# Attention scores by three 64-row products per head, in the two halves of TensorE's array

## The chip, the core and the metric

The program runs on one NeuronCore of a Trainium2 chip. TensorE (PE) multiplies matrices: the stationary operand is loaded into its array of 128 rows and columns by a weight load (PEld), and the moving operand streams past, one column at a time. VectorE (DVE), ScalarE (ACT) and GpSimd (POOL) work elementwise, SyncE (SP) issues transfers. The metric is device time in microseconds (us) of one execution of the whole program; lower is better.

## What is computed

One step of a two-layer decoder trunk on 1024 prompt tokens and 8 sample tokens, width 1024. The first layer mixes tokens by dilated window attention: three groups g with window and dilation (128, 1), (512, 4), (2048, 16), 16 heads of 64 each; the groups are merged per head by their softmax denominators. Then come a gated channel mixer, a pooling mixer, and a second channel mixer; neither these nor the samples' attention change. What the change touches is this, per block of 128 queries of a residue stream:

```python
s = jnp.einsum("nbqhd,nbkhd->nbhqk", qb, kb).astype(jnp.float32) * SCALE
s = s + bias[:, np.clip(rel, 0, SPAN)]
s = jnp.where(valid[None, :, None], s, NEG_INF)
m = jnp.max(s, axis=-1)
p = jnp.exp(s - m[..., None])
l = jnp.sum(p, axis=-1)
o = jnp.einsum("nbhqk,nbkhd->nbqhd", p.astype(v.dtype), vb).astype(jnp.float32)
```

A block of queries reads the keys of its own block and, where there is one, of the block before.

## The kernel before

All matrix products are made of rounded parts: an operand is split into its rounded value and the rest, and three products (value by value, value by rest, rest by value) are added in PSUM.

`order` lists 24 **units**, a pair of heads (hp) in a group (g), pair by pair with g = 2, 1, 0. While a unit's queries, keys and values are projected, the attention of the unit before runs in between. The projections of a unit are nine groups of 24 products of 336 to 352 columns (`accumulate`, L116), three chunks of tokens for each of queries, keys and values. Behind every third product `between` is called; it moves a clock on by one place, 72 in a unit, and issues the steps of the list `plan` that have come due. So the order on each engine is fixed when the program is written: a step's instructions stand on every engine's queue in the order of the places, and an instruction that waits holds up all behind it on that engine. `attend` puts block i's scores at place 6i+1, the transposes of its weights (`probs_t`) at 6i+15, weights times values (`pv`) at 6i+24, and `finish_o` two places behind each second block. Steps of the sample tokens and of the merge of the groups (`behind`, `extra`) lie between these.

- `evacuate` (L353 on) copies a projected chunk from PSUM to the tile `raw` on ScalarE (L362), queries scaled by 1/8, in the order of the residue streams.
- `pack_q` (L384) makes of a head's queries a tile of 128 rows: rounded values in the head's own 64 rows and their rests in the other 64. `pack_k` (L398) makes a tile of keys twice over and, beside it, keys' rests over 64 rows of zeros. Both are copies and subtractions of 64 partitions by 512, on ScalarE, VectorE and GpSimd, at places 29 to 46.5 and 50 to 59.
- `scores` (L441): a **narrow** block (no block before it; 13 of the 24 blocks of a pair) is one product per head of 256 columns (keys, and keys' rests; L450), and VectorE adds the two halves and the bias (L451). A **wide** block is two products per head of 256 columns, added in PSUM (L457). Then VectorE adds the rest and takes the row maximum (L459), negates it (L461), and ScalarE takes the exponential (L463). The scores of both heads share one bank of PSUM (`s`).
- `probs_t` transposes the weights into one bank (`pt`, L471, L473); ScalarE rounds them (L475) and VectorE takes the rest (L476).
- `pv_mm` (L483) streams the weights' two parts in one product of 256 or 512 columns per head, into columns of their own; two of the three banks `o` hold the two heads of a pair of blocks. `finish_o` waits for ScalarE's copy across partitions (L501), adds on VectorE (L510), and GpSimd adds the two parts into token order (L518).

## Time and profile before

| | us |
|---|---|
| median of 3 runs (lowest to highest) | 3011.26 (3010.56 to 3012.93) |
| span of the profiled execution | 3007.3 |
| of it TensorE busy | 2796.5 |
| VectorE busy | 1649.7 |
| ScalarE busy | 1273.2 |
| GpSimd busy | 1241.8 |

The span runs from the first to the last instruction; the 4 us between it and the median lie around it. Matmul records overlap, as a product's end is modelled with its way through the array; what a product costs in a stream is read from one start to the next. A row "X <- Y" of waits says that X's engine sat idle until Y was done.

### The profile page before, as it was taken

Reading aid. Unit: us, or ns where it says so; the run is one execution under the profiler, and the core shown is the slowest. Engines: PE = TensorE matmul, PEld = TensorE weight load, DVE = VectorE, ACT = ScalarE, POOL = GpSimd, SP = SyncE. Lnnn points to the kernel's source line nnn. Section 1 sums busy time; section 2 is a strip of 40 time slices with the busy share of each in tenths; the row PEclk is TensorE's granted clock in tenths of the full one; section 3 lists DMA queues with packets and bytes.
Section 4 is the critical chain, followed back from the end, with each engine's and each line's share of the span. In section 5 each row is a group of like instructions: output and inputs, shape, how many; then the busy total and the mean of one; then the engine's idle time right before and its main releaser. Section 6 shows DMA issues by size and latency. Waiting matters only on the chain.

```text
span 3007.3 us, 45367 instructions
## 1 busy us (share of the span) xinstructions
PE 2796.5 (93%) x17677; PEld 2724.2 (91%) x17677; DVE 1649.7 (55%) x3338; ACT 1273.2 (42%) x2596; POOL 1241.8 (41%) x949
## 2 busy tenths in 40 slices
PE   7998999998989898899999999998797999999998
PEld 5988888888989798889999999998787999999998
DVE  6677767676777767766222222337977422223235
ACT  5565656565656555544312122224454221312222
POOL 4345554555354636444423232336543532323231
PEclk9999999999999999999999999999898999999999
DMA  3134332433232324356111111113225211111111
GB/s 114 54 86 115 82 85 78 109 100 89 70 111 82 103 54 127 130 146 54 63 44 50 44 48 50 47 66 110 88 88 60 90 50 43 50 50 43 50 43 60
DMA packets 190119, 227.38 MB, mean 76 GB/s; under 512 B 68736, under 2 KB 152560, under 8 KB 189904
## 3 DMA queue, kind: packets, MB, share of 16 engines
q1 hardware_dynamic: 189856, 224.47, 26.9%
q8 instruction: 139, 2.28, 0.3%
q14 instruction: 76, 0.62, 0.1%
q10 hardware_dynamic: 48, 0.02, 0.0%
HBM read 201.55 MB, written 23.34 MB: 75 GB/s over the span
## 4 chain that ended last, share of the span: by engine, by line
PE 50%; DVE 10%; ACT 2%; issue 2%; DMA 1%; POOL 1%; SPq 0%; DVEq 0%; ACTq 0%; POOLq 0%
PE mm L116 49%; DVE nm L461 1%; DVE conv L1108 1%; POOL w_lo L96 1%; DVE sums L1217 1%; DVE part L211 1%; DMA w_raw<-in_w_in 1%; DVE p L459 0%; DVE nrow L239 0%; ACT w_hi L95 0%; DVE hl L251 0%; DVE x L393 0%; ACT p L463 0%; DVE k L402 0%; DVE phl L476 0%
## 5 line engine op out<-in xcount | busy, mean ns | idle before, releaser
L116 PE MATMUL mm<-hh,w_hi 128*128 128x352 f32 (+2 forms) x4064 | 1347.5, 332 | 29.4 <-DVE conv L1099 9.7
L116 PE MATMUL mm<-hh,w_lo 128*128 128x352 f32 (+2 forms) x4064 | 1316.5, 324 | 5.7 <-POOL w_lo L96 5.5
L116 PE MATMUL mm<-hl,w_hi 128*128 128x352 f32 (+2 forms) x4064 | 1318.3, 324 | 3.4 <-DVE hl L251 3.2
L116 PEld LDWEIGHTS mm<-hh,w_hi 128*128 128x128 f32 x4064 | 780.6, 192 | 40.3 <-DVE conv L1099 10.2
L116 PEld LDWEIGHTS mm<-hl,w_hi 128*128 128x128 f32 x4064 | 780.6, 192 | 10.5 <-DVE hl L251 6.8
L116 PEld LDWEIGHTS mm<-hh,w_lo 128*128 128x128 f32 x4064 | 779.2, 192 | 7.2 <-POOL w_lo L96 7.2
L96 POOL TENSOR_TENSOR w_lo<-w_raw,w_hi 128x1024 fp32r<-128x1024 f32 x194 | 478.2, 2466 | 530.7 <-ACT w_hi L95 515.4
L1108 DVE SCALAR_TENSOR_TENSOR conv<-gate,convp,conv 128x1024 f32<-128x1024 f32 (+3 forms) x126 | 135.0, 1072 | 474.8 <-ACT conv L1106 463.2
L116 PE MATMUL mm<-gh,w_hi 128*128 128x352 f32 (+2 forms) x1056 | 338.8, 321 | 7.8 <-ACT gh L1100 7.6
L116 PE MATMUL mm<-gl,w_hi 128*128 128x352 f32 (+2 forms) x1056 | 339.0, 321 | 1.2 <-POOL gl L1101 1.2
L116 PE MATMUL mm<-gh,w_lo 128*128 128x352 f32 (+2 forms) x1056 | 338.5, 321 | 0.2 <-POOL w_lo L96 0.2
L1044 DVE TENSOR_TENSOR x<-x,mm 128x352 f32<-128x352 f32 (+2 forms) x312 | 159.0, 511 | 309.0 <-PE mm L116 308.8
L95 ACT ACTIVATE w_hi<-w_raw 128x1024 fp32r<-128x1024 f32 x196 | 205.5, 1051 | 242.4 <-PE mm L116 231.3
L463 ACT ACTIVATE p<-p,nm 128x128 f32<-128x128 f32 (+1 forms) x384 | 169.8, 443 | 296.3 <-DVE nm L461 286.1
L1101 POOL TENSOR_TENSOR gl<-conv,gh 128x352 fp32r<-128x352 f32 (+2 forms) x132 | 122.5, 939 | 269.4 <-ACT gh L1100 267.6
L116 PEld LDWEIGHTS mm<-gh,w_hi 128*128 128x128 f32 x1056 | 199.2, 189 | 8.6 <-ACT gh L1100 8.1
L96 POOL TENSOR_TENSOR w_lo<-part,w_hi 128x1024 fp32r<-128x1024 f32 x56 | 138.2, 2468 | 151.5 <-ACT w_hi L95 142.1
L116 PEld LDWEIGHTS mm<-gl,w_hi 128*128 128x128 f32 x1056 | 199.0, 188 | 1.8 <-POOL gl L1101 1.8
L476 DVE TENSOR_TENSOR phl<-pt,phl 128x512 fp32r<-128x512 f32 (+1 forms) x192 | 104.6, 545 | 173.8 <-ACT phl L475 172.5
L116 PEld LDWEIGHTS mm<-gh,w_lo 128*128 128x128 f32 x1056 | 199.2, 189 | 0.5 <-POOL w_lo L96 0.5
L362 ACT ACTIVATE raw<-mm 128x336 f32<-128x336 f32 (+1 forms) x216 | 144.2, 669 | 118.4 <-PE mm L116 115.8
L1090 ACT ACTIVATE gate<-mm 128x352 f32<-128x352 f32 (+2 forms) x132 | 60.0, 455 | 299.6 <-PE mm L116 299.6
(195 smaller groups left out, 3467.6 us busy)
## 6 DMA issues: line engine op xcount, KB each, us to landing
w_raw<-in_w_in SPq DMA_DIRECT2D x76, 512.0 KB
w_raw<-in_w_qkv SPq DMA_DIRECT2D x72, 512.0 KB
part<-in_w_in SPq DMA_DIRECT2D x38, 512.0 KB
w_raw<-in_w_out SPq DMA_DIRECT2D x36, 512.0 KB
x<-qd SPq DMA_DIRECT2D x48, 256.0 KB
kc<-in_cache_k SPq DMA_DIRECT2D x48, 256.0 KB
vc<-in_cache_v SPq DMA_DIRECT2D x48, 256.0 KB
x<-c_d SPq DMA_DIRECT2D x42, 256.0 KB
```

The lines of the kernel that those rows point to most:

```text
L95: nc.scalar.activation(hi, raw, AF.Copy)
L96: (eng or nc.gpsimd).tensor_sub(lo, raw, hi.bitcast(F32))
L116: nc.tensor.matmul(ps, l, r, start=first and i == 0, stop=last and i == n - 1)
L211: self.engines[j].tensor_add(acc, acc, s[:, :self.w])
L362: nc.scalar.activation(stream(raw[:, :T], u.g, c0, t1, which > 0), ps[:, :w].rearrange("p (s r) -> p s r", r=DILS[u.g]), AF.Copy, scale=scale)
L461: nc.vector.tensor_scalar(nm, u.st[:, i, :, 0], -1.0, None, op0=ALU.mult)
L463: nc.scalar.activation(p[:, h, :w], p[:, h, :w], AF.Exp, bias=nm[:, h:h + 1], accum_out=u.st[:, i, h, 1:2])
L476: nc.vector.tensor_sub(phl[:, :, 1, :w], ps[:, :, :w], phl[:, :, 0, :w].bitcast(F32))
L1044: nc.vector.tensor_add(xT[ct][:, c0:c1], xT[ct][:, c0:c1], ps)
L1090: nc.scalar.activation(gate[:, 2 + s:2 + e], group(tiles8(w, c), c), AF.Copy)
L1101: nc.gpsimd.tensor_sub(self.gl[f][:, s:e], conv[:, s:e], self.gh[f][:, s:e].bitcast(F32))
L1108: nc.vector.scalar_tensor_tensor(conv[:, c0:t1], gate[:, j + c0:j + t1], cw[j], conv[:, c0:t1], op0=ALU.mult, op1=ALU.add)
```

## The change

The tile of keys becomes one for both heads: 128 partitions, that is 64 of each head, with values and rests side by side. Queries are no longer packed: `evacuate` writes the rounded, negated queries from PSUM on ScalarE and their rests from PSUM on VectorE, straight into a pair of tiles, of which there are two (`queries`, `other_queries`) for odd and even units. A block's scores are three products per head of 64 rows, head A in rows 0 to 63 of the array and head B in rows 64 to 127, in turn, each head into a bank of its own. Scores, bias table and masks are negated, so that the reduction takes a minimum and the exponential a scale of -1; L451 and L461 go. `pv_mm` adds the weights' two parts in PSUM, as two products of half the columns; both heads share one bank and two banks take turns; `finish_o` adds on VectorE straight into token order, and GpSimd's addition goes. Banks of PSUM: `s` from one to two, `o` from three to two.

The program has as many transfers on SyncE's queue as before. The diff, without lines that only change comments, placeholders of the norms' banks, or line numbers:

```diff
-        keys = [qp.tile([128, 2, T], F32R, name=f"k{h}") for h in range(2)]
+        keys = qp.tile([128, 2, T], F32R, name="k")
+        other_queries = qp.tile([128, 2, T], F32R, name="q")
+        queries = []
...
-                    nc.vector.tensor_add(masks[g], ps, masks[g])
+                    nc.vector.scalar_tensor_tensor(masks[g], ps, -1.0, masks[g], op0=ALU.mult, op1=ALU.subtract)
...
-            nc.scalar.activation(stream(raw[:, :T], u.g, c0, t1, which > 0),
-                                 ps[:, :w].rearrange("p (s r) -> p s r", r=DILS[u.g]), AF.Copy, scale=scale)
+            src = ps[:, :w].rearrange("p (s r) -> p s r", r=DILS[u.g])
+            if which == 0:
+                hi, lo = (stream(raw[x], u.g, c0, t1, False) for x in range(2))
+                nc.scalar.activation(hi, src, AF.Copy, scale=-scale)
+                nc.vector.scalar_tensor_tensor(lo, src, -scale, hi.bitcast(F32), op0=ALU.mult, op1=ALU.subtract)
+            else:
+                nc.scalar.activation(stream(raw[:, :T], u.g, c0, t1, True), src, AF.Copy)
...
-        def pack_q(u):
-            raw = u.raw[0]
-            if not queries:
-                queries.extend(x_row(h, F32R)[:, :T] for h in range(2))
-
-            def part(h, own, other, t):
-                (nc.vector.tensor_copy(queries[h][own, t], raw[own, t]) if h else
-                 nc.scalar.activation(queries[h][own, t], raw[own, t], AF.Copy))
-                (nc.vector if h else nc.gpsimd).tensor_sub(queries[h][other, t], raw[own, t],
-                                                           queries[h][own, t].bitcast(F32))
-
-            return parts(part, (0, T // 2))
-
         def pack_k(u):
             raw = u.raw[1]
 
-            def part(h, own, other, t):
-                nc.vector.tensor_copy(keys[h][own, 0, t], raw[own, t])
-                nc.scalar.activation(keys[h][other, 0, t], raw[own, t], AF.Copy)
-                (nc.vector if h else nc.gpsimd).tensor_sub(keys[h][own, 1, t], raw[own, t],
-                                                           keys[h][own, 0, t].bitcast(F32))
-
-            return parts(part, (T // 2, 0))
-
-        def parts(f, starts):
-            return [partial(f, h, own, other, slice(t, t + T // 2)) for t in starts
-                    for h, (own, other) in enumerate(((A, B), (B, A)))]
-
+            def part(eng, t):
+                nc.scalar.activation(keys[:, 0, t], raw[:, t], AF.Copy)
+                eng.tensor_sub(keys[:, 1, t], raw[:, t], keys[:, 0, t].bitcast(F32))
+            return [partial(part, nc.vector, slice(T // 2, T)), partial(part, nc.gpsimd, slice(0, T // 2))]
...
-            ps = app.tile([128, 2, 2, 128], F32, name="s", tag="s")
+            ps = [app.tile([128, 256], F32, name="s", tag="s", bufs=2)[:, :w] for h in range(2)]
             p = qp.tile([128, 2, 256], F32, name="p", tag="p", bufs=4)
-            nm = qp.tile([128, 2], F32, name="nm", tag="nm", bufs=2)
-            if w == 128:
-                for h in range(2):
-                    nc.tensor.matmul(ps[:, h], queries[h][:, q], keys[h][:, :, k], start=True, stop=True)
-                nc.vector.tensor_add(p[:, :, :w], ps[:, :, 0], u.bias[:, :, :w])
-                s, bias = ps[:, :, 1], p
-            else:
-                s, bias = ps.rearrange("p h a q -> p h (a q)"), u.bias
-                for h in range(2):
-                    for x in range(2):
-                        nc.tensor.matmul(s[:, h], queries[h][:, q], keys[h][:, x, k], start=x == 0, stop=x == 1)
+            for j, (x, y) in enumerate(((0, 0), (0, 1), (1, 0))):
+                for h, own in enumerate((A, B)):
+                    nc.tensor.matmul(ps[h], u.raw[0][x][own, q], keys[own, y, k], start=j == 0, stop=j == 2)
             for h in range(2):
-                nc.vector.tensor_tensor_reduce(p[:, h, :w], s[:, h, :w], bias[:, h, :w], 1.0, -3e38,
-                                               op0=ALU.add, op1=ALU.max, accum_out=u.st[:, i, h, 0:1])
-            nc.vector.tensor_scalar(nm, u.st[:, i, :, 0], -1.0, None, op0=ALU.mult)
+                nc.vector.tensor_tensor_reduce(p[:, h, :w], ps[h], u.bias[:, h, :w], 1.0, 3e38,
+                                               op0=ALU.add, op1=ALU.min, accum_out=u.st[:, i, h, 0:1])
             for h in range(2):
-                nc.scalar.activation(p[:, h, :w], p[:, h, :w], AF.Exp, bias=nm[:, h:h + 1],
+                nc.scalar.activation(p[:, h, :w], p[:, h, :w], AF.Exp, bias=u.st[:, i, h, 0:1], scale=-1.0,
                                      accum_out=u.st[:, i, h, 1:2])
...
-                nc.tensor.matmul(u.o[h][:, :, 128 * q:128 * (q + b1 - b0)], u.v[j // 4][:, j % 4, h, :],
-                                 u.pt[j][0][:, h, :, 128 * b0:128 * b1], start=first, stop=True, skip_group_check=True)
+                for x in range(2):
+                    nc.tensor.matmul(u.o[:, h, 128 * q:128 * (q + b1 - b0)], u.v[j // 4][:, j % 4, h, :],
+                                     u.pt[j][0][:, h, x, 128 * b0:128 * b1], start=first and h + x == 0, stop=True,
+                                     skip_group_check=True)
...
-                u.o = [app.tile([128, 2, 256], F32, name="o", tag="o", bufs=3) for h in range(2)]
+                u.o = app.tile([128, 2, 256], F32, name="o", tag="o", bufs=2)
...
-                x = 512 * (j // 2 % 2)
-                tmp = (part[:, 0, x:x + 512].rearrange("p (x q) -> p x q", x=2) if (u.hp, u.g) != order[23] else
-                       qp.tile([128, 2, 256], F32, name="ot", tag="ot", bufs=1))
+                x = 256 * (j // 2 % 2)
+                tmp = (part[:, 0, x:x + 256] if (u.hp, u.g) != order[23] else
+                       qp.tile([128, 256], F32, name="ot", tag="ot", bufs=1))
                 u.tmp = tmp, u.o
                 for h, (own, other) in enumerate(((A, B), (B, A))):
-                    nc.scalar.activation(u.tmp[0][own], u.o[h][other], AF.Copy)
+                    nc.scalar.activation(tmp[own], u.o[other, h], AF.Copy)
...
             tmp, o = u.tmp
+            if u.g == 0:
+                dst, split = u.og[:, 256 * i:256 * i + 256], lambda t: t
+            elif u.g == 1:
+                dst = u.og.rearrange("p (n q r) -> p r n q", n=2, r=4)[:, i]
+                split = lambda t: t.rearrange("p (n q) -> p n q", n=2)
+            else:
+                dst = u.og.rearrange("p (s r) -> p r s", r=16)[:, 4 * i:4 * i + 4]
+                split = lambda t: t.rearrange("p (n q) -> p n q", n=4)
             for h, own in enumerate((A, B)):
-                nc.vector.tensor_add(tmp[own], o[h][own], tmp[own])
-            if u.g == 0:
-                dst, split = u.og[:, 256 * i:256 * i + 256], "p q -> p q"
-            elif u.g == 1:
-                dst, split = u.og.rearrange("p (n q r) -> p r n q", n=2, r=4)[:, i], "p (n q) -> p n q"
-            else:
-                dst, split = u.og.rearrange("p (s r) -> p r s", r=16)[:, 4 * i:4 * i + 4], "p (n q) -> p n q"
-            parts = [tmp[:, x] if u.g == 0 else tmp[:, x].rearrange(split, n=2 if u.g == 1 else 4) for x in range(2)]
-            nc.gpsimd.tensor_add(dst, *parts)
-
+                nc.vector.tensor_add(dst[own], split(o[own, h]), split(tmp[own]))
...
-                nc.vector.tensor_max(mx, top[:, 0], top[:, 1])
-                nc.vector.tensor_max(mx, mx, top[:, 2])
-                nc.vector.tensor_sub(e, top, each(mx))
+                nc.vector.tensor_tensor(mx, top[:, 0], top[:, 1], op=ALU.min)
+                nc.vector.tensor_tensor(mx, mx, top[:, 2], op=ALU.min)
+                nc.vector.tensor_sub(e, each(mx), top)
...
-                        self.rooms = [[keys[x][:, :, t:t + 256] for x in range(2)] for t in (768, 512)]
+                        self.rooms = [[other_queries[:, x, t:t + 512].rearrange("p (b d) -> p b d", b=2) for x in range(2)]
+                                      for t in (0, 512)]
...
-                    u.raw.append(qp.tile([128, NT], F32, name="raw", tag="raw", bufs=RAW))
+                    if which:
+                        u.raw.append(qp.tile([128, NT], F32, name="raw", tag="raw", bufs=RAW))
+                    elif n % 2:
+                        if not queries:
+                            queries.extend(x_row(x, F32R)[:, :T] for x in range(2))
+                        u.raw.append(queries)
+                    else:
+                        u.raw.append([other_queries[:, x] for x in range(2)])
...
-                if n and i in (2, 5):
-                    places = (29, 29 + 3, 44.5, 44.5 + 2) if i == 2 else [50 + 3 * j for j in range(4)]
-                    plan.extend(zip(places, pack_q(u) if i == 2 else pack_k(u)))
+                if n and i == 5:
+                    plan.extend(zip((50, 53), pack_k(u)))
```

Two places show the order. On TensorE, in the attention of a unit of g = 0, from the values of one block to the scores of the next; o are weights times values, s scores, pt transposed weights, mm the projection. Before:

```order
L483 MATMUL o<-phl,vhl 128x2x128 x2
L116 MATMUL mm<-hh,w_hi 128x352
L116 MATMUL mm<-hl,w_hi 128x352
L116 MATMUL mm<-hh,w_lo 128x352
L457 MATMUL s<-k_100,x_593 128x256 x2
L457 MATMUL s<-k_101,x_594 128x256 x2
L116 MATMUL mm<-hh,w_hi 128x336
L116 MATMUL mm<-hl,w_hi 128x336
L116 MATMUL mm<-hh,w_lo 128x336
```

and after:

```order
L463 MATMUL o<-phl,vhl 128x128 x4
L116 MATMUL mm<-hh,w_hi 128x352
L116 MATMUL mm<-hl,w_hi 128x352
L116 MATMUL mm<-hh,w_lo 128x352
L436 MATMUL s<-k,q 128x256 x6
L116 MATMUL mm<-hh,w_hi 128x336
L116 MATMUL mm<-hl,w_hi 128x336
L116 MATMUL mm<-hh,w_lo 128x336
```

The steps stand at the same places between the same large products; two products of the values have become four of half the columns, and four of the scores six with 64 rows.

On VectorE, in the attention of a unit of g = 2, where the next unit's queries (x) and keys (k) are packed from raw; phl are rests of the weights, part and o the sums of the values, ks the samples' keys. Before:

```order
L365 TENSOR_SCALAR ks_98<-mm_4336 128x8
L391 CAST x1_594<-raw_3983 64x512
L393 TENSOR_TENSOR x1_594<-raw_3983,x1_594 64x512
L402 CAST k0_100<-raw_4174 64x512
L476 TENSOR_TENSOR phl_4427<-pt_4424,phl_4427 128x2x128
L402 CAST k1_101<-raw_4174 64x512
L404 TENSOR_TENSOR k1_101<-raw_4174,k1_101 64x512
L510 TENSOR_TENSOR part_65<-o_4408,part_65 64x512
L510 TENSOR_TENSOR part_65<-o_4409,part_65 64x512
```

and after:

```order
L373 TENSOR_SCALAR ks_98<-mm_4384 128x8
L396 TENSOR_TENSOR k_100<-raw_4217,k_100 128x512
L454 TENSOR_TENSOR phl_4474<-pt_4471,phl_4474 128x2x128
L499 TENSOR_TENSOR x6_4319<-o_4455,part_65 64x4x64 x2
L454 TENSOR_TENSOR phl_4516<-pt_4513,phl_4516 128x2x128
L499 TENSOR_TENSOR x6_4319<-o_4528,part_65 64x4x64 x2
```

The copies and rests of queries and keys ahead of the rests of the weights (phl) have left this place but for one subtraction of keys; the sums of the values write the output row (x6) themselves. The queries' rests stand earlier, behind each chunk of the queries' projection.

## Rows read from the trace of the kernel before

**Rows 1.** The page's part 1, the whole span: busy us of each engine (share of the span) xinstructions.

```profile
PE 2796.5 (93%) x17677; PEld 2724.2 (91%) x17677; DVE 1649.7 (55%) x3338; ACT 1273.2 (42%) x2596; POOL 1241.8 (41%) x949
```

**Rows 2.** The stretch in which attention runs beside the products of the projections, 60 to 1330 us: busy time of each engine with its count of instructions in brackets, the granted clock of TensorE as a share, the share of DMA and GB/s; and, of the same stretch, the longest waits of TensorE: who waited for whom, us in total, times, longest us.

```profile
60.00:1330.00 1270.00, 1144.76 (x7349) 1089.72 (x7349) 910.53 (x2175) 737.78 (x1766) 612.52 (x418) 0.97 0.34 94
...
PE pt L471 <- DVE phl L476: 37.6, 35, 2.6
PE o L483 <- DVE part L510: 37.5, 23, 3.3
PE spv L760 <- DVE so L787: 14.2, 10, 2.5
```

**Rows 3.** The same view of two units' stretches: one that carries steps of the sample tokens, and the one behind it, which carries none.

```profile
691.80:745.70 53.90, 45.65 (x298) 42.45 (x299) 39.24 (x89) 30.82 (x76) 33.36 (x20) 1.00 0.31 78
745.70:792.50 46.80, 45.01 (x297) 43.65 (x297) 32.29 (x74) 27.10 (x70) 15.89 (x12) 1.00 0.16 45
```

**Rows 4.** TensorE's groups of instructions, whole span, shapes kept apart: stationary x moving shape, count | busy us, mean ns of one | idle before. L450 and L457 are scores, L483 is weights times values.

```profile
L450 PE MATMUL s<-k,x 128*128 128x256 f32 x208 | 42.7, 286 | 3.0 <-POOL k L404 2.9
L457 PE MATMUL s<-k,x 128*128 128x256 f32 x352 | 56.1, 281 | 1.3 <-DVE st L459 1.3
L483 PE MATMUL o<-phl,vhl 128*128 128x256 f32 x304 | 68.3, 293 | 31.2 <-DVE part L510 30.6
L483 PE MATMUL o<-phl,vhl 128*128 128x512 f32 x128 | 43.2, 409 | 6.8 <-DVE part L510 6.8
```

**Rows 5.** Pieces of TensorE's order of time in a unit without samples: start us, us (of a merged row, of all of it), engine, line, operation. The first piece is a narrow block of scores between large products, the second four transposes, the third weights times values and then a wide block of scores.

```profile
756.00 0.32 PE L116 MATMUL mm<-hh,w_lo 128*128 128x352 f32 x1
756.16 0.40 PE L450 MATMUL s<-k,x 128*128 128x256 f32 x2
756.39 0.33 PE L116 MATMUL mm<-hh,w_hi 128*128 128x352 f32 x1
756.56 0.32 PE L116 MATMUL mm<-hl,w_hi 128*128 128x352 f32 x1
...
758.13 0.32 PE L116 MATMUL mm<-hh,w_lo 128*128 128x352 f32 x1
758.29 0.60 PE L434 MATMUL vt<-consts,raw 128*128 128x128 f32 x4
758.64 0.41 PE L116 MATMUL mm<-hh,w_hi 128*128 128x352 f32 x1
758.89 0.33 PE L116 MATMUL mm<-hl,w_hi 128*128 128x352 f32 x1
...
759.54 0.32 PE L116 MATMUL mm<-hh,w_lo 128*128 128x352 f32 x1
759.71 0.40 PE L483 MATMUL o<-phl,vhl 128*128 128x256 f32 x2
759.94 0.32 PE L116 MATMUL mm<-hh,w_hi 128*128 128x352 f32 x1
760.10 0.32 PE L116 MATMUL mm<-hl,w_hi 128*128 128x352 f32 x1
760.26 0.32 PE L116 MATMUL mm<-hh,w_lo 128*128 128x352 f32 x1
760.42 0.63 PE L457 MATMUL s<-k,x 128*128 128x256 f32 x4
760.89 0.31 PE L116 MATMUL mm<-hh,w_hi 128*128 128x336 f32 x1
761.04 0.32 PE L116 MATMUL mm<-hl,w_hi 128*128 128x336 f32 x1
```

**Rows 6.** Order of time around four small products of 16 rows (L783), the only ones of this stretch that use a part of the array's rows: weight loads (PEld) and products (PE), with the large products ahead and behind.

```profile
391.44 0.32 PE L116 MATMUL mm<-hh,w_lo 128*128 128x344 f32 x1
391.68 0.52 PEld L783 LDWEIGHTS spt<-selm,spv_sb 16*128 16x128 f32 x4 [0.21 <-issue]
...
392.22 0.19 PEld L116 LDWEIGHTS mm<-hh,w_hi 128*128 128x128 f32 x1
392.22 0.42 PE L116 MATMUL mm<-hh,w_hi 128*128 128x344 f32 x1
392.32 0.19 PEld L116 LDWEIGHTS mm<-hl,w_hi 128*128 128x128 f32 x1
...
392.48 0.31 PE L116 MATMUL mm<-hl,w_hi 128*128 128x344 f32 x1
```

**Rows 7.** From the same piece of time, a GpSimd instruction and a VectorE one.

```profile
391.83 2.35 POOL L594 TENSOR_TENSOR x<-x,x 128x1024 f32<-128x1024 f32 x1
...
392.32 1.88 DVE L461 TENSOR_SCALAR nm<-st 128x2 f32<-128x2 f32 x1
```

**Rows 8.** VectorE's costliest groups in the stretch of 60 to 1330 us that the diff touches, shapes kept apart: count | busy us, mean ns of one | idle before.

```profile
L510 DVE TENSOR_TENSOR part<-o,part 64x512 f32<-64x512 f32 x184 | 126.2, 686 | 7.1 <-ACT part L501 3.8
L461 DVE TENSOR_SCALAR nm<-st 128x2 f32<-128x2 f32 x192 | 107.3, 559 | 6.7
L402 DVE CAST k<-raw 64x512 fp32r<-64x512 f32 x96 | 79.4, 828 | 2.3
L393 DVE TENSOR_TENSOR x<-raw,x 64x512 fp32r<-64x512 f32 x48 | 71.0, 1479 | 1.6
L404 DVE TENSOR_TENSOR k<-raw,k 64x512 fp32r<-64x512 f32 x48 | 67.6, 1408 | 1.6
```

More of the change, by code (lines that the diff above doesn't have):

```diff
@@ L302, in place @@
             banks.rotate(1)
-            return app.tile([128, 512], F32, name="nstat", tag=banks[0], bufs=3 if banks[0] == "o" else 1)
+            return app.tile([128, 512], F32, name="nstat", tag=banks[0], bufs=2 if banks[0] in "os" else 1)
         nc.scalar.activation(warm, ones, AF.Sqrt)
-        banks = deque(["o", "o", "pt", "misc", "o", "s"])
+        banks = deque(["o", "o", "pt", "misc", "s", "s"])
         load_x(0)
@@ L326, in step @@
             def step(g, tag, src):
-                ps = app.tile([16, TAB], F32, name="btp", tag=tag)
+                ps = app.tile([16, TAB], F32, name="btp", tag=tag, bufs=2 if tag == "s" else 1)
                 ps = ps[:, :src.stop - src.start]
@@ L353, in trunk @@
         class Unit:
+            pass
         def evacuate(u, which, ps, c):
@@ L936, in trunk @@
                             b2 = qp.tile([128, 2, 128], F32, name=f"bias2_{x}")
-                            nc.gpsimd.memset(b2, NEG)
+                            nc.gpsimd.memset(b2, -NEG)
                             bias2.append(b2)
@@ L940, in trunk @@
                         nc.gpsimd.memset(zero, 0.0)
-                        for h, other in enumerate((B, A)):
-                            nc.scalar.activation(keys[h][other, 1], zero[other].to_broadcast([64, T]), AF.Copy)
                         nc.scalar.activation(pst.rearrange("p g b c -> p (g b c)"), zero.to_broadcast([128, 48 * NS]), AF.Copy)
@@ L954, in trunk @@
                         later(f, .8)
-                if n == 0 and i in (6, 7):
+                if n == 0 and i == 7:
                     nc.scalar.activation(warm, ones, AF.Exp)
-                    for f in pack_q(u) if i == 6 else pack_k(u):
+                    for f in pack_k(u):
                         later(f, .6)
```

1 line of the change is left out of this document (removed).

## Prediction

> **What bounds the kernel now.** First the page's busy times: TensorE is busy in 93% of the span and VectorE in little over half [rows 1], so the end is set by TensorE's queue: a step is worth what it puts on that queue or how long it makes it wait. The diff touches only the stretch with attention, so I read that next. Of its 1270 us TensorE is busy 1144.8 and idle 125.2, with a granted clock of 0.97; the longest waits are all for VectorE: transposes wait until the rests of the weights before them have left their bank (37.6), values wait for a free sum bank (37.5), samples' products wait 14.2 [rows 2]. VectorE is busy 72% of this stretch, more than its share of the whole. Then units beside each other: one with samples' steps idles 8.25 of 53.9 us, the next, without them, 1.8 of 46.8 us at clock 1.00, though VectorE is busy 69% in it too [rows 3]. So the kernel here is TensorE's stream plus VectorE's queueing. The change trades one for the other: it takes much from VectorE and adds products to TensorE.
>
> **Prices on TensorE's queue.** I read a step's price from starts: from the large product ahead to the second one behind, less the two large products themselves (0.31 to 0.33). Then a narrow block of scores, two products of 256 columns, costs 0.24; four transposes of 128 columns 0.44; the values, twice 256 columns, 0.24; a wide block, four products of 256, 0.46 [rows 5]. A product of 128 columns thus takes 0.11 and one of 256 only 0.12: with few columns the weight load sets the pace. The load's own length says so too: the four of 16 rows run in 0.52 together, one each 0.11, whether or not rows are filled [rows 6]. Streaming 256 columns more adds 0.116 to a product (409 against 293 ns [rows 4]), so 128 columns stream in 0.06.
>
> **Weights times values.** 304 products of 256 columns (152 pairs) [rows 4] become 608 of 128, each paced by its load: 608 x 0.11 - 152 x 0.24 = +30.4 us. 128 products of 512 become 256 of 256: four at 0.12 are 0.48 against 2 x (0.12 + 0.116) = 0.47, +0.6. Together **+31**, all of it on TensorE's queue, since the large products leave no hole.
>
> **Scores.** 208 / 2 = 104 narrow blocks and 352 / 4 = 88 wide ones [rows 4] become six products each. No row shows 64 rows of the array. The nearest are the four small products of 16 rows: the first load starts 0.24 after the large product ahead, which otherwise is followed after 0.16, and the first large product behind starts only with its own load, 0.26 ahead of the next [rows 6]. In all the four cost 392.48 - 391.44 - 0.31 = 0.73, of which four loads are 0.44: **0.29 is the price of going over to part of the array and back**, and the last product then also has to stream before the array is given back (0.06 or 0.12). I take 0.29 for 64 rows, the nearest row; the other end is 0, if it came from those few rows alone.
>
> What the trace doesn't show is whether two halves load and stream side by side. At one end the six products are three turns: narrow 3 x 0.11 + 0.06 + 0.29 = 0.68, wide 3 x 0.11 + 0.12 + 0.29 = 0.74, that is 104 x 0.44 + 88 x 0.28 = +70 us. At the other end they are six: narrow 1.01, wide 1.07, or 104 x 0.77 + 88 x 0.61 = +134. I take **+70**: the two halves share no row of the array, no partition they read and no bank they write, and in the rows a load waits only for another load into the same rows. The Trainium skill (TensorEngine Tiling (Array Packing), section Tiling Modes) says that different tiles can load weights and multiply in parallel; by that the sum is the one I take, else the 64 us more of the six turns, and no run here shows it.
>
> **VectorE, ScalarE and GpSimd.** Gone from VectorE in this stretch: sums of the values 126.2, negated maxima 107.3, keys 79.4 and 67.6, queries' rests 71.0 [rows 8], 451 us, and with them smaller copies and additions. The negated maxima are 128 x 2 elements; their mean of 559 ns is mostly waiting. One of them lasts 1.88 us and ends at 394.20, as the GpSimd instruction that began before it ends at 394.18 [rows 7]. That work comes back smaller: 192 sums of half the columns (0.34 to 0.69 each by the 686 ns of L510, 66 to 131 us), 72 rests of queries (at most 0.69, so 50), 24 rests of keys (at most 1.41, so 34). VectorE loses some 240 to 350 of its 910.5 us and falls from 72% to about half of the stretch. ScalarE loses copies and GpSimd packing and final sums; neither is waited for above. SyncE's queue keeps its transfers.
>
> **What the waits give back.** The idle time is 125.2. A quiet unit keeps 1.8 [rows 3]; 24 such are 43, the one end, and 0 the other. I keep 35, near the quiet unit, which still had the old VectorE work: **-90** (-82 to -125). The wait for a sum bank should go wholly, since a bank now waits two pairs of blocks for its turn. Late next are the samples' chains through one bank and back, whose steps stay. The clock: 0.97, a mean of its two levels of 2.4 and 1.2 GHz, over 1270 us [rows 2] withholds 38 us of full clock, the quiet unit gets 1.00; part of the withheld time is itself idle, so **-22** (-10 to -38). The queries' new rests add a wait: a bank of the projection is free only after ScalarE and then VectorE have read it. Behind that subtraction stand the next blocks' row maxima and rests of weights. TensorE has two such banks and fills one in 24 products of 0.16, 3.8 us, which covers two reads of under 0.8; I cost it at nothing. If that cover is gone and each of the 72 chunks waits for one VectorE instruction of 0.69 [rows 8], that is 50 us, within the range below.
>
> **Sum.** +31 + 70 - 90 - 22 = -11. The profiled span is 3007.3; the median 3011.26 has 4 us more around it, and these don't change. Predicted time **3000 us**. By its own bounds this case reaches from 2950 (waits and clock given back in full) to 3025 (least given back, some of the bank's wait).
>
> **Rivals.**
> 1. *Six turns:* the halves load one behind the other, as each load does in every row so far [rows 5, 6]. +31 + 134 - 112 = +53: **3064**, slower. It decides the sign from where a pair takes more than 0.13 us (11 us over 192 x 3 pairs is 0.02 each). For it: every load shown has a turn of its own. Against it: all of these are loads into the same rows.
> 2. *No price for the change of array part:* 192 blocks x 0.29 = 56 us less than the forecast: **2944**. For it: the 0.29 is read from products of 16 rows and 4 columns alone. Against it: its two gaps lie outside those products, one ahead and one behind.
> 3. *A load can't run under a product in its own rows:* then each of the three turns is load and stream in series, narrow 3 x 0.17 + 0.29 = 0.80, wide 3 x 0.23 + 0.29 = 0.98; 104 x 0.56 + 88 x 0.52 = 104 us: +31 + 104 - 112 = +23, **3034**. Against it: the load at 392.32 starts while the large product of 392.22 runs in the same 128 rows [rows 6]. The Trainium skill (TensorE: Matmul & The Clock Gate, section Part 3: Packing small matmuls — row/col tiling) says that a load overlaps products in flight only where the row groups differ, which would give this time; for full rows the row here speaks against it.
> 4. *The waits stay:* the idle time hangs on the chain from ScalarE's rounding to VectorE's rests more than on VectorE's load, and only half of the 112 comes back: +31 + 70 - 56 = +45, **3056**. For it: an unloaded chain also takes two engines. Against it: the same chain in a quiet unit idles 1.8 us.
>
> **How the numbers follow.** Forecast 0.47, six turns 0.25, no price 0.14, load in series 0.07, waits stay 0.07. Measurements of this kernel can tell about 0.2%, 6 us, from no change. The forecast, at -11 with some 20 us to either side, holds 0.29 faster, 0.10 same, 0.08 slower; no price is 0.14 faster; six turns are 0.02, 0.01, 0.22; load in series 0.01, 0.01, 0.05; waits stay 0.01, 0.01, 0.05. Sums: faster 0.47, same 0.13, slower 0.40. The range of 2938 to 3064 leaves out half of the six turns and a little below: under 2 in 10. The likeliest case's own range is 2950 to 3025.
>
> **What would show it.** In the profile after: six score products whose two halves start a few hundredths apart, in pairs 0.11 to 0.12 apart, are three turns; even steps of 0.11 are six. A gap of 0.1 ahead of the first score load and a large product of 0.26 behind the last are the price of the change. Four products of the values should cost 0.44. TensorE's idle time in the stretch should fall to some 35 us, its waits for the sum bank to nothing, VectorE to about half, the clock to 0.99. I am wrong if pairs take 0.2 us, if idle time stays over 80 us, or if `mm` waits for the queries' rests.

## The result, and the profile after

| | before | after |
|---|---|---|
| median, us (runs) | 3010.91 (4) | 2941.85 (4) |
| lowest to highest | 3004.15 to 3012.93 | 2940.03 to 2943.78 |
| span of the profiled execution | 3007.3 | 2940.4 |

The ratio is 0.9767, 95% interval 0.9748 to 0.9785: 69 us faster. The forecast was 3000, 11 us faster than before; its sign held, but five sixths of the gain were not in the sum. The range held the time by luck: 2941.85 lies below the forecast's own bounds (2950 to 3025), and the range went lower only for a rival, *no price*, whose mechanism the runs refute.

The page's part 1, of after, beside [rows 1]:

```profile
PE 2841.9 (97%) x18701; PEld 2744.1 (93%) x18701; DVE 1320.8 (45%) x2898; ACT 1182.9 (40%) x2497; POOL 1063.7 (36%) x781
```

TensorE is busy 45 us longer in a span that is 67 us shorter. Behind the attention both kernels have 1677 us left (1330 to 3007, 1263 to 2940), so all of it lies in the stretch of [rows 2]. The same stretch after: busy time of each engine, clock, DMA.

```profile
60.00:1263.00 1203.00, 1193.06 (x8381) 1112.59 (x8380) 581.62 (x1734) 649.62 (x1669) 434.68 (x250) 1.00 0.37 100
```

TensorE's waits, whole span after, those that lie in the stretch and concern steps of the change or of the samples; the last is for the bank that the queries' rests now read. In the changed kernel L436 are the scores, L463 weights times values, L449 the transposes, L454 the rests of the weights, L743 samples' products and L369 the queries' rests.

```profile
PE pt L449 <- DVE phl L454: 2.8, 4, 0.7
...
PE spv L743 <- DVE so L770: 2.1, 4, 0.6
...
PE mm L116 <- DVE q L369: 0.8, 1, 0.8
```

Idle time falls from 125.2 us to 9.9, the clock rises from 0.97 to 1.00, and VectorE goes from 910.5 to 581.6 us, from 72% to 48% of the stretch. The wait for a sum bank, 37.5 us before, is not listed any more; transposes wait 2.8 us for the rests of weights, 37.6 before.

TensorE's order of time, after: a narrow block of scores with the large products around it; then weights times values and a wide block.

```profile
671.25 0.32 PE L116 MATMUL mm<-hh,w_lo 128*128 128x344 f32 x1
671.50 0.55 PE L436 MATMUL s<-k,q 64*128 64x128 f32 x6
671.98 0.43 PE L116 MATMUL mm<-hh,w_hi 128*128 128x344 f32 x1
672.24 0.32 PE L116 MATMUL mm<-hl,w_hi 128*128 128x344 f32 x1
...
728.25 0.32 PE L116 MATMUL mm<-hh,w_lo 128*128 128x352 f32 x1
728.41 0.56 PE L463 MATMUL o<-phl,vhl 128*128 128x128 f32 x4
728.80 0.38 PE L116 MATMUL mm<-hh,w_hi 128*128 128x352 f32 x1
729.02 0.32 PE L116 MATMUL mm<-hl,w_hi 128*128 128x352 f32 x1
729.18 0.32 PE L116 MATMUL mm<-hh,w_lo 128*128 128x352 f32 x1
729.43 0.62 PE L436 MATMUL s<-k,x 64*128 64x256 f32 x6
729.98 0.42 PE L116 MATMUL mm<-hh,w_hi 128*128 128x336 f32 x1
730.24 0.32 PE L116 MATMUL mm<-hl,w_hi 128*128 128x336 f32 x1
```

By the method of [rows 5] a narrow block costs 672.24 - 671.25 - 0.31 = 0.68, a wide one 730.24 - 729.18 - 0.32 = 0.74, four values 729.02 - 728.25 - 0.32 = 0.45. The first score load comes 0.25 behind the large product instead of 0.16, and the large product behind the block keeps its successor waiting 0.26. Six products take 0.48 from first start to the next large product: single records in the trace show the two halves' loads in pairs, 671.495 and 671.499, 671.604 and 671.607, 671.713 and 671.716.

**Where the 67 us come from.** For each small group on TensorE (scores, transposes, values, samples' products) I take the time from the large product ahead to the second one behind, less two large products. The lower quartile over groups of the same make-up is its *price*; what groups take above that, and what large products take above their median, is the *excess*: waits and low clock. In the stretch:

| | before | after | difference |
|---|---|---|---|
| large products at their median | 830.9 | 832.0 | +1 |
| price of the small groups | 261.9 | 359.9 | +98 |
| excess of the small groups | 155.0 | 7.8 | -147 |
| excess of the large products | 21.8 | 3.0 | -19 |

Before, the excess of small groups is 30 us more than the 125.2 us of listed idle time: a product's end is modelled with its way through the array, so a wait that begins under that tail is listed short. Two rows of before show it:

```profile
701.24 0.32 PE L116 MATMUL mm<-hh,w_lo 128*128 128x344 f32 x1
703.17 0.63 PE L760 MATMUL spv<-x,pst 128*16 128x256 f32 x4 [1.61 <-DVE so L787]
```

The waiting product starts 1.77 later than the usual 0.16 behind the large one, and 1.61 of idle time are listed for it. TensorE sits idle 121 times in the stretch; 0.16 for each is 19 of the 30 us. The rest was not taken apart; low clock among the small products is one part of it.

VectorE's groups in the same stretch, beside [rows 8]: count | busy us, mean ns of one | idle before.

```profile
L499 DVE TENSOR_TENSOR x<-o,part 64x256 f32<-64x256 f32 x184 | 101.9, 554 | 46.5 <-ACT part L482 44.9
...
L396 DVE TENSOR_TENSOR k<-raw,k 128x512 fp32r<-128x512 f32 x24 | 50.5, 2103 | 31.2 <-ACT k L395 31.2
...
L369 DVE SCALAR_TENSOR_TENSOR x<-mm,x 128x336 fp32r<-128x336 f32 x24 | 16.5, 686 | 20.2 <-ACT x L368 20.2
```

The sums stay, cheaper; one subtraction of keys takes 2.1 us, where the prediction had at most 1.41, but TensorE's waits above have no row for it; the negated maxima, 107.3 us before, have no row.

### The profile page after: what moved, and what is told of

It reads as the page before. It is cut to its first block, busy times and chain, and to the rows that moved or that the text cites. A ratio compares the mean times of both kernels' runs of the same rounds, so it can differ in the third digit from the quotient of the medians.

```text
span 2940.4 us, 46741 instructions
## 1 busy us (share of the span) xinstructions
PE 2841.9 (97%) x18701; PEld 2744.1 (93%) x18701; DVE 1320.8 (45%) x2898; ACT 1182.9 (40%) x2497; POOL 1063.7 (36%) x781
## 4 chain that ended last, share of the span: by engine, by line
PE 87%; DVE 7%; ACT 2%; issue 2%; DMA 1%; POOL 1%; SPq 0%; DVEq 0%; ACTq 0%; POOLq 0%
PE mm L116 76%; PE s L436 3%; PE o L463 3%; PE pt L449 1%; DVE sums L1204 1%; DVE nrow L239 1%; DVE conv L1095 1%; PE vt L420 1%; PE spv L743 1%; PE pt L451 1%; DVE part L211 1%; DMA w_raw<-in_w_in 1%; DVE hl L251 1%; ACT w_hi L95 0%; POOL w_lo L96 0%
## 5 line engine op out<-in xcount | busy, mean ns | idle before, releaser
L116 PE MATMUL mm<-hh,w_hi 128*128 128x352 f32 (+2 forms) x4064 | 1361.2, 335 | 30.1 <-DVE conv L1086 9.7
L116 PEld LDWEIGHTS mm<-hh,w_hi 128*128 128x128 f32 x4064 | 771.4, 190 | 54.6 <-DVE conv L1086 10.2
L116 PEld LDWEIGHTS mm<-hl,w_hi 128*128 128x128 f32 x4064 | 772.3, 190 | 7.6 <-DVE hl L251 6.9
L116 PEld LDWEIGHTS mm<-hh,w_lo 128*128 128x128 f32 x4064 | 770.9, 190 | 8.3 <-POOL w_lo L96 8.3
L441 ACT ACTIVATE p<-p,st 128x128 f32<-128x128 f32 (+1 forms) x384 | 169.6, 443 | 201.5 <-DVE st L438 201.5
L438 DVE CUSTOM_DVE_ANT_0 p<-s,bias 128x128 f32<-128x128 f32 (+1 forms) x384 | 119.8, 349 | 174.7 <-PE s L436 174.1
L454 DVE TENSOR_TENSOR phl<-pt,phl 128x512 fp32r<-128x512 f32 (+1 forms) x192 | 104.6, 545 | 145.4 <-ACT phl L453 143.1
```

The lines of the kernel that those rows point to most:

```text
L116: nc.tensor.matmul(ps, l, r, start=first and i == 0, stop=last and i == n - 1)
L438: nc.vector.tensor_tensor_reduce(p[:, h, :w], ps[h], u.bias[:, h, :w], 1.0, 3e38, op0=ALU.add, op1=ALU.min, accum_out=u.st[:, i, h, 0:1])
L441: nc.scalar.activation(p[:, h, :w], p[:, h, :w], AF.Exp, bias=u.st[:, i, h, 0:1], scale=-1.0, accum_out=u.st[:, i, h, 1:2])
L454: nc.vector.tensor_sub(phl[:, :, 1, :w], ps[:, :, :w], phl[:, :, 0, :w].bitcast(F32))
```

## The experiments

All were timed in three rounds beside the kernel before. "Price" is that of the small groups in the stretch, "excess" that of small groups and large products together.

| kernel | ratio, 95% interval | price | excess |
|---|---|---|---|
| before | 1 | 262 | 177 |
| after | 0.9767 [0.9748, 0.9785] | 360 | 11 |
| 1 scores negated alone | 0.9832 [0.9816, 0.9848] | 262 | 128 |
| 2 sums in PSUM alone | 0.9912 [0.9893, 0.9932] | 297 | 116 |
| 3 both, old scores and packing | 0.9724 [0.9705, 0.9743] | 295 | 62 |
| 4 after, halves in series | 0.9777 [0.9761, 0.9792] | 361 | 10 |
| 5 after, minima copied | 0.9851 [0.9836, 0.9866] | 365 | 34 |
| 6 after, full rows | 0.9766 [0.9751, 0.9781] | 360 | 11 |
| 7 after, blocks in twos | 0.9686 [0.9671, 0.9700] | 329 | 19 |
| 8 as 3, second `pt` bank | 0.9762 [0.9746, 0.9779] | 295 | 75 |
| 9 after, minima copied from PSUM | 0.9764 [0.9743, 0.9784] | 360 | 10 |
| 10 as 3, keys rounded on ScalarE | 0.9612 [0.9594, 0.9629] | 294 | 31 |
| 11 before, negation in PSUM form | 0.9858 [0.9840, 0.9876] | 262 | 132 |
| 12 as 10, queries too | 0.9622 [0.9607, 0.9637] | 295 | 32 |

My theory (L) was that the waits went because VectorE lost work, wherever that work stood; the rivals, that the sum banks (B) or the packing of queries and keys (H) did it.

**1. Scores negated alone**, on the kernel before; the copy of the maxima goes.

```diff
-            nc.vector.tensor_scalar(nm, u.st[:, i, :, 0], -1.0, None, op0=ALU.mult)
-                nc.scalar.activation(p[:, h, :w], p[:, h, :w], AF.Exp, bias=nm[:, h:h + 1],
+                nc.scalar.activation(p[:, h, :w], p[:, h, :w], AF.Exp, bias=u.st[:, i, h, 0:1], scale=-1.0,
```

> Kernel before with the negated scores alone (row minimum, no separate negation on VectorE); packing, 128-row scores and sums as before. Theory L (TensorE waited because VectorE was full): VectorE loses the 107 us of L461 and ScalarE no longer waits for it, TensorE's queue is unchanged, so a good third of the 177 us that waits and low clock cost goes: 2940 to 2975 us. Rival B (TensorE waited for the sum banks and the banks behind them, whatever VectorE's load): under 15 us, 2996 or more.

2960.25 us, 50 faster, as L expected. The two longest waits of TensorE that are left in the stretch are these; the one for a sum bank is as long as in the kernel before (37.5 there), that of the transposes is shorter (37.6 there):

```profile
PE o L481 <- DVE part L508: 38.7, 20, 3.9
PE pt L469 <- DVE phl L474: 21.2, 27, 1.5
```

**2. Sums in PSUM alone**: `pv_mm`, `finish_o` and two banks `o`, as in the change.

> Kernel before with the sums of the values alone changed (two products of half the columns added in PSUM, both heads in one bank, two banks in turn, final addition on VectorE). TensorE's queue grows by 31 us. Theory L: VectorE's load falls by only some 50 us; the bank's wait (37.5) and little else goes: 2985 to 3020 us. Rival B: most of the 177 us goes, 31 come: 2890 to 2920 us.

2983.37 us, 28 faster, a little below L's range and far above B's: 35 more of price, 61 less of excess. The wait for a sum bank has no row left.

**3. Both of these**, with the scores and the packing of before.

> Both parts together on the kernel before: everything of the change but the scores in halves, the query split from PSUM and the keys over 128 partitions. TensorE's queue has 31 us more instead of 101. Theory L: VectorE falls from 72% to about 60% of the stretch, some two thirds of the 177 us go: 2915 to 2945 us, that is no slower than the whole change, because 70 us of score products are saved while some waits stay. Rival H (the packing of queries and keys is what filled VectorE; without its removal the waits stay): 2970 us or more.

2927.61 us: faster than the whole change, and the excess that goes (114) is the sum of the two parts' (49 and 61) within 4 us. H falls: the rest of the change, scores in halves and the new packing, puts 65 us of price on TensorE's queue and takes 52 of excess away. By this it costs 13 us; the times differ by 14.

**4. Halves in series.** After, with three products of head A, then three of head B.

```diff
-            for j, (x, y) in enumerate(((0, 0), (0, 1), (1, 0))):
-                for h, own in enumerate((A, B)):
+            for h, own in enumerate((A, B)):
+                for j, (x, y) in enumerate(((0, 0), (0, 1), (1, 0))):
```

> Changed kernel with a block's six products in the order A A A B B B instead of A B A B A B; the same products, banks and reads. If the halves' loads and products run side by side only when they alternate, and TensorE's queue has no slack left, each block takes six turns of 0.11 us instead of three: +0.33 us x 192 = +64, 3000 to 3010 us. Rival: order doesn't matter, as loads are drawn ahead or as three turns aren't what sets the pace: 2942 us.

2943.06 us, as after. I expected the turn-taking to be what lets the halves run side by side; the rival holds. The six take no longer in TensorE's order of time:

```profile
671.99 0.32 PE L116 MATMUL mm<-hh,w_lo 128*128 128x344 f32 x1
672.24 0.56 PE L436 MATMUL s<-k,q 64*128 64x128 f32 x6
672.72 0.43 PE L116 MATMUL mm<-hh,w_hi 128*128 128x344 f32 x1
672.99 0.32 PE L116 MATMUL mm<-hl,w_hi 128*128 128x344 f32 x1
```

Single records again show pairs, loads at 672.234 and 672.244, 672.342 and 672.353, 672.452 and 672.462. A record does not name its half; loads into the same rows start 0.10 apart or more in all rows shown.

**5. Minima copied.** After, with 192 small copies between minimum and exponential, in the form of the removed negation.

```diff
+            nc.vector.tensor_scalar(nm, u.st[:, i, :, 0], 1.0, None, op0=ALU.mult)
```

> Changed kernel with a small VectorE instruction put back in every block: the row minima are copied before the exponential reads them, 192 instructions of 128 x 2 like those that were removed (107 us of VectorE before). Theory L (VectorE's queue has room now, TensorE's queue alone sets the pace): under 8 us, 2942 to 2950. Rival: each such instruction costs what it did before, some 50 us by the run with the negation alone: 2985 to 2995 us.

2966.54 us, 25 more than after: the time lies between the two expectations, and both miss. The copies (the view of one line; ns are minimum, median, maximum) take 0.17 us at best and 115.0 us in all, a mean of 599 ns:

```profile
L441 DVE TENSOR_SCALAR nm<-st x192: 169/170/2383, 73.6 to 1257.1; 128x2 f32<-128x2 f32 x192
```

**6. Full rows.** After, with all six products over the 128 rows, so that each head's scores contain the other's too.

```diff
-                    nc.tensor.matmul(ps[h], u.raw[0][x][own, q], keys[own, y, k], start=j == 0, stop=j == 2)
+                    nc.tensor.matmul(ps[h], u.raw[0][x][:, q], keys[:, y, k], start=j == 0, stop=j == 2)
```

> Changed kernel with each of a block's six products over all 128 rows instead of 64: a head's scores then contain the other head's too, so the output is another one, with the same number of products, columns, banks and reads behind them. If the halves' gain (three turns instead of six, -0.33 to -0.36 us) and the price of going over to part of the array (0.29) cancel, as the sum has them, the blocks cost 0.66 and 0.71 instead of 0.68 and 0.75: 2935 to 2943 us. Rival: the price is smaller than the gain: 2955 us or more.

2942.52 us, as after. The order of time shows what is traded:

```profile
671.16 0.32 PE L116 MATMUL mm<-hh,w_lo 128*128 128x344 f32 x1
671.32 0.78 PE L436 MATMUL s<-k,q 128*128 128x128 f32 x6
671.93 0.37 PE L116 MATMUL mm<-hh,w_hi 128*128 128x344 f32 x1
672.14 0.32 PE L116 MATMUL mm<-hl,w_hi 128*128 128x344 f32 x1
```

No gap ahead (0.16), 0.61 instead of 0.48 for the six, 0.21 instead of 0.26 behind: 0.67 against 0.68. What two halves side by side save is what going over to them and back costs.

**7. Blocks in twos.** After, with the scores of two blocks issued together, twelve products in a row, so that the change of array part is paid half as often.

> Changed kernel with the scores of two blocks issued together, so that the array is given over once for twelve products instead of twice for six; the same products, both blocks of a head in one bank. If 0.29 us is paid per going over and back and the last product's stream is exposed once, each pair of blocks saves about 0.35 us, 96 x 0.35 = 34 us: 2903 to 2915 us. Rival P (the price belongs to the products, not to the going over): 2940 us; rival W (one turn of both banks makes waits for the row minima): above 2942 us.

2918.01 us, 24 faster than after and 3 above the expected range. The price falls by 31 (96 changes of array part fewer, at 0.29, are 28); 8 come back as excess.

**8. A second `pt` bank** for the kernel of experiment 3 (`bufs=2` for that tag).

> Negated scores and new sums on the kernel before, scores over 128 rows as before, and the bank of PSUM that this leaves free given to the transposed weights (two in turn). TensorE's queue as in the run without it; the waits of the transposes for the rests of the weights (10 us seen as idle, more with their exposed loads) go: 2905 to 2922 us. Rival: these waits only move to the products behind them: 2924 us or more.

2940.98 us, 13 slower than experiment 3. There the values and the transposes wait for the rests of the weights:

```profile
PE o L483 <- DVE phl L474: 12.3, 10, 2.2
PE pt L469 <- DVE phl L474: 10.0, 14, 1.4
```

With the second bank the transposes' wait is gone from the list, and the values behind them wait longer:

```profile
PE o L483 <- DVE phl L474: 21.7, 10, 4.5
```

So the bank only moved the wait, 22 us in all in both kernels. The 13 us are not idle time. The stretch of experiment 3 and then that of 8, as in [rows 2]:

```profile
60.00:1250.00 1190.00, 1141.72 (x7795) 1111.71 (x7794) 777.46 (x1986) 704.81 (x1766) 536.58 (x322) 0.99 0.37 102
60.00:1262.00 1202.00, 1152.49 (x7791) 1126.43 (x7790) 777.37 (x1984) 707.28 (x1766) 535.67 (x322) 0.98 0.36 100
```

TensorE idles 48.3 and 49.5 us, but its busy time is 10.8 longer, with a granted clock of 0.98 instead of 0.99; the excess of the large products goes from 9 to 20 us. That the longer single waits, up to 4.5 us instead of 2.2, brought the clock down is likely and not shown.

**9. Minima copied from PSUM.** As 5, the same numbers from an instruction that also reads two scores and multiplies them by 0.

```diff
+            nc.vector.scalar_tensor_tensor(nm, ps[0][:, 0:2], 0.0, u.st[:, i, :, 0], op0=ALU.mult, op1=ALU.add)
```

> Changed kernel with the same small VectorE instruction per block as in the run with the minima copied, but in a form that reads one operand from PSUM (0 x score + minimum), as the instructions do whose length never varied in the traces. Theory G (the 25 us of that run are the instruction's waits for GpSimd's instructions, 0.6 us in the mean instead of 0.17): it takes 0.2 us every time and the kernel 2942 to 2950 us. Rival C (one more link between row minimum and exponential costs that, whatever its length): 2958 to 2968 us.

2942.17 us, as after. The copies in the same view:

```profile
L441 DVE SCALAR_TENSOR_TENSOR nm<-s,st x192: 159/159/163, 74.1 to 1228.3; 128x2 f32<-128x2 f32 x192
```

So neither the further step nor the 31 us on VectorE costs anything here; the 25 us of experiment 5 are the long ones among its copies.

**10. Keys rounded on ScalarE**, in the kernel of experiment 3.

```diff
-                nc.vector.tensor_copy(keys[h][own, 0, t], raw[own, t])
+                nc.scalar.activation(keys[h][own, 0, t], raw[own, t], AF.Copy)
```

> Negated scores and new sums on the kernel before, with the rounding of the keys (96 copies of 64 x 512, 86 us) moved from VectorE to ScalarE. Theory L: VectorE's long instructions with both operands in SBUF get fewer, a third of the remaining 62 us of waits goes: 2900 to 2918 us. Rival A (ScalarE, with 60 us more, becomes what the chains wait for): 2925 us or more.

2896.27 us, 31 faster than experiment 3, just below what L expected, and the best of all. It takes from VectorE 96 copies, the first group of experiment 3's:

```profile
L402 DVE CAST k<-raw 64x512 fp32r<-64x512 f32 x96 | 105.7, 1101 | 2.2
```

The shortest of these copies takes 0.41 us; 96 of that length are 39 us, so most of the 105.7 is waiting. Whether the gain comes from the work or from these waits was not tried apart.

**11. The negation of before, in PSUM form.** The kernel before, with this in place of L461.

```diff
-            nc.vector.tensor_scalar(nm, u.st[:, i, :, 0], -1.0, None, op0=ALU.mult)
+            nc.vector.scalar_tensor_tensor(nm, ps[:, 0, 0, 0:2], 0.0, u.st[:, i, :, 0], op0=ALU.mult, op1=ALU.subtract)
```

> The kernel before with its 192 negations of the maxima left in their place, but in a form that reads the scores' bank of PSUM beside the maxima (0 x score - maximum, the same numbers). Theory G, that the 50 us which leaving them out gave came from their waits for GpSimd's instructions and not from the instructions: each lasts some 0.16 us, as in the changed kernel, VectorE gives up some 75 us, and the time is that of the kernel without negations, 2955 to 2968. Rival C, that a further step between minimum and exponential costs, or the room it takes on VectorE: 2990 or more.

2967.89 us: ratio 0.9858, against 0.9832 without any negation. Of that gain of 1.7% the form alone gives 1.4%. The negations of before and then of this run, in the view of one line:

```profile
L461 DVE TENSOR_SCALAR nm<-st x192: 169/170/2307, 79.9 to 1295.6; 128x2 f32<-128x2 f32 x192
L461 DVE SCALAR_TENSOR_TENSOR nm<-s,st x192: 158/159/163, 80.0 to 1251.3; 128x2 f32<-128x2 f32 x192
```

Before, 62 of the 192 take longer than 0.23 us. Each of these began while a GpSimd instruction ran and ended within 0.06 us of its end. In this run 63 begin under a GpSimd instruction that runs on, and none is longer than 0.163.

**12. Queries rounded on ScalarE too**, in the kernel of experiment 10 (the copy of head B's queries, like head A's).

> The best version so far (negated scores, sums added in PSUM, keys rounded on ScalarE) with head B's queries rounded on ScalarE as well, 48 instructions of 0.80 us on VectorE. Theory V, that what is left of the waits is still queueing on VectorE: 2880 to 2893, with VectorE at some 655 of the stretch's 1204 us and the excess of TensorE's steps under 25 us. Rival S, that ScalarE (777 of 1204 us, with these some 815) is the engine that is waited for by now, as its rounding stands ahead of the weights' rests: 2896 to 2915.

2897.88 us, the same as experiment 10 within the intervals, so theory V, which is L once more, fails and S gave the time. VectorE lost 23 us in the stretch (664.7 to 641.9) and the excess stayed the same (31 and 32); VectorE now waits for ScalarE ahead of the queries' rests. Experiment 10 and then this one:

```profile
L393 DVE TENSOR_TENSOR x<-raw,x 64x512 fp32r<-64x512 f32 x48 | 45.7, 952 | 1.6
L392 DVE TENSOR_TENSOR x<-raw,x 64x512 fp32r<-64x512 f32 x48 | 45.8, 954 | 31.1 <-ACT x L391 30.9
```

## Why the prediction was right or wrong, point by point

**TensorE's prices: right.** Values and scores were to add 31 + 70 = 101; the price rose by 98. By experiment 3, 33 of that belong to the values and 65 to the scores. Narrow 0.68, wide 0.74 and values 0.44 were read at 0.68, 0.74 and 0.45.

**Two halves side by side: right**, so *six turns* falls: pairs start 0.004 apart and 0.11 behind each other. The order of the six, which the prediction did not weigh, makes no difference (experiment 4).

**The change of array part: right at 0.29**, read from four products of 16 rows. (They are not the only ones of the stretch on a part of the rows, as [rows 6] has it: L713, L728 and L329 use 32.) *No price* gave 2944, near the time, but for a wrong reason: both gaps are there, experiment 7 saves what the price says when half the changes go, and experiment 6 shows that the halves gain no more than it. The rival *load in series* falls by the same prices, and *waits stay* by the 9.9 us of idle time that are left.

**The clock: right.** -22 forecast, -19 measured: large products lost 21.8 us before, nearly all in low clock, and 3.0 after, with a granted clock of 0.97 and 1.00.

**What the waits give back: the term that was mis-sized.** -90 forecast, -147 measured, which is all of the miss. VectorE's own fall was forecast well, 329 us of 240 to 350. Two parts of the term were wrong. I kept 35 us of listed idle time, by a quiet unit's 1.8; 9.9 stayed, 0.4 a unit. That quiet unit still had VectorE's old work, and I used it as a floor for a kernel without it. And I took the wait's cost from the idle time listed, though I had measured prices from starts: by starts the small groups' excess, waits with their share of low clock, was 155 us, 30 more. Put into the sum, -147 and -19 give +98 - 166 + 1 = -67.

**Why so much goes: the cause that the prediction named in passing.** It said that the negated maxima's mean of 559 ns "is mostly waiting" and counted them as 107 us of work among 451. Of the parts tried alone they give the largest gain, 50 us against 28 for the sums; of the excess they take 49, the sums 61. In [rows 7] one ends with the GpSimd instruction that began before it, and so do all 62 long ones; without such waits the instruction takes 0.17 us, in the other form 0.16. They stand between maximum and exponential, so they hold up the transposes, and VectorE's queue behind them holds up the rests and sums; which of the two counts more was not tried apart. Changing only the instruction's form on the kernel before gives 43 us (experiment 11), bringing the waits back into the changed kernel costs 25 (5), and an instruction in the same place without them costs nothing (9). So L holds only in part: as far as these three go, it was not the work that VectorE lost but the waiting within it. The Trainium skill (SBUF — State Buffer, section Who interferes with whom) says that VectorE and GpSimd share a pair of ports which whoever issues first holds for its whole instruction, that an operation on scalars can run in a mode that takes the pair, and that a VectorE instruction with at most one input from SBUF, outside such modes, does not contend. The rows agree: a maximum of 2383 ns in one form, of 163 in the other.

**The sum banks: right in size.** The 37.5 us went. With VectorE lighter by 84 us in experiment 1 this wait stayed (38.7), so relief alone doesn't remove it. Experiment 2 takes it, and 61 us of excess in all, with two banks in turn and VectorE's lighter sums together; which of the two does it was not tried apart.

**Packing and scores: the part that I costed as a trade loses.** What the halves and the new packing put on TensorE (65) is more than the excess they remove beside the other two parts (52): experiment 3 is faster than the change. From there on a cheaper way to free VectorE was one line of rounding (experiment 10), and experiment 12 marks where that ends: with VectorE lighter still (642 us) and ScalarE busier (795 instead of 762), nothing more comes back. What the last 31 us of excess in experiment 10 wait for, I did not settle.

**The queries' new rests: right at nothing**, one wait of 0.8 us on their bank.

## What to carry to other kernels

An instruction whose mean is several times its shortest is a wait with a name: look which engine's instruction ends with it, and try another form (an operand in PSUM) before moving work. On a full queue price a wait, like a step, from starts, and never use a stretch that still carries the old load as the floor for one without it. When a change bundles parts, run the parts: here two of the three beat the whole, since the third paid more in TensorE's own time than it took from the waits.

## What the runs showed of the hardware that was not expected

- Products of the two halves of the array run beside each other even where those of the second half stand behind all three of the first in the program (experiment 4, starts 0.01 us apart). The Trainium skill (TensorE: Matmul & The Clock Gate, Part 3: Packing small matmuls — row/col tiling) says that products start and end in program order, with no reordering; these records, which stand in pairs, do not agree.
- A second bank for the transposes made the kernel 13 us slower (experiment 8) with hardly more idle time (48.3 and 49.5 us): single waits became longer, up to 4.5 us instead of 2.2, and the granted clock was 0.98 instead of 0.99.
- A VectorE instruction of 128x2 lasted 0.17 to 2.31 us in one form and never more than 0.163 in the other, with about as many begun beside a GpSimd instruction (62 long ones and 63, experiment 11).
